# Remainder splits of the value and gate operands moved from GpSimd (POOL) to VectorE (DVE) in a two-layer decoder trunk

## The chip, the cores and the metric

The kernel runs on one core of one Trainium2 chip. The metric is the device time of one execution in microseconds (us). Engines are named as the profile names them: PE is TensorE (matmul), PEld its weight load, DVE is VectorE, ACT is ScalarE, POOL is GpSimd, SP is SyncE, which issues most DMAs. For a run of this kernel, about 0.3% (some 5.3 us) is what a measurement can tell from no change.

## The reference

The input x is 1024 tokens by 1024 features, float32. Layer 0 is an RWKV-7 time mixing, layer 1 a differential attention; each is followed by a gated per-layer embedding, and one RMSNorm ends the trunk. What matters here, cut down:

```
h = rms_norm(x);  dx = token_shift(h) - h
xm[g] = h + dx * mu[g]                      # g = r, k, v, gate
r, k, v, gate = xm[g] @ w_in[g]             # 1024x1024 each
...                                         # decay, per-head state update, group norm
x = x + (y * silu(gate)) @ w_out
x = x + sigmoid(rms_norm(x) @ pe_w_gate[0]) * (p[0] @ pe_w_proj[0])
...                                         # layer 1: differential attention
x = x + sigmoid(rms_norm(x) @ pe_w_gate[1]) * (p[1] @ pe_w_proj[1])
out = rms_norm(x)
```

## The kernel before

A matmul here is made of three in a shortened float type (float32r): an operand a is split into a main part (a rounded to float32r) and a remainder (a minus the main part), and a·b is taken as main·main + main·remainder + remainder·main (`mm3`, L90). `split` (L86) makes both: ACT writes the main part, and then POOL, or DVE where the caller says so, subtracts to get the remainder.

The work around the change, in order of time:

- **Mixed operands.** `make_xm` (L251) makes one 128x512 piece of xm[g]: ACT or DVE scales hT into a scratch tile `xmt` (a ring of 3), DVE adds the shifted part, `split` writes main part and remainder. There are 16 pieces for each g (8 feature blocks kt by 2 token halves). In the code g counts 1 for k, 0 for r, 2 for v, 3 for the gate. The remainder goes to DVE for kt 1, 4, 7 of v and kt 1 of the gate, and else to POOL.
- **Weights.** `wload` (L267) fetches a 128x1024 row of weights and splits it, always with POOL. The names are wv00 to wv31 for the 8 rows of v, and w0_, w1_, w3_ for the 8 rows each of r, k and the gate (w3_ is the gate; the profile prints these as w_0 to w_7).
- **Dense products.** `dense_T` (L274) makes k, then r; the loop at L681 makes v (4 column quarters by 8 token tiles, tiles `v`), and `dense_T` again makes the gate (tiles `d`). At the end of each dense product the operands of the next are made.
- **The inverse beside v and gate.** `inv_steps` (L646) runs in the background of v and gate. For four quarters q it makes products `pb` on PE, scales them on DVE (`nq`), transposes them on DVE (`nb`), and then does 31 steps of two DVE instructions each, one after the other (`tm`, then `tb`); two DVE transposes (`ea`, `ti`), copies on ACT (`prhs`, `pairs`) and small PE products (`pg`, `po`) end it.
- **The state update and layer 1** follow (from about 565 us); the order on the engines is pinned there by hand, and the edits do not touch it.
- **The last stage.** While layer 1's output projection runs (tiles `do`), `gate_pair` (L1551) fetches the 8 rows of the last gate's weights (pwg10 to pwg17) through `gate_row` (L761) and `wrow` (L743). Each row is scaled by a norm weight. With an engine given, `wrow` scales the raw row in place on ACT, then splits it: ACT main part, that engine the remainder. With none, ACT makes the main part with the scale in one instruction, and DVE makes the remainder with the scale in one instruction (SCALAR_TENSOR_TENSOR). The last token tile's chain (`os`, `ost`, `o`, `g`) runs beside it, and then the last gate's products (`fg`) begin.

Outside the pinned part the order of the instructions on each engine is set when the kernel is built, by a planner that simulates the program; each engine then runs its own list in order. Raw weight rows go through rings of two tiles, so the fetch of a row waits until the remainder two rows before it is made.

Of the kernel before, what the change touches and what calls it, by code (L numbers as in the profile page):

```python
# [37 lines left out]
def trunk(ctx: ExitStack, tc: tile.TileContext, A, out):  # L38
# [17 lines left out]
    V, S, G, T = engines = [Engine(e) for e in (nc.vector, nc.scalar, nc.gpsimd, nc.tensor)]  # L56
# [29 lines left out]
    def split(hi, lo, src, lo_eng=None):  # L86
        S.activation(hi, src, AF.Copy)
        (lo_eng or G).tensor_tensor(out=lo, in0=src, in1=hi.bitcast(F32), op=ALU.subtract)
# [132 lines left out]
    with NB("ab") as ab, NP("psab") as pp:  # L221
# [18 lines left out]
        def xslot(nm, n=512):  # L240
            return (ab.tile([P, 513], F32R, tag="xmh", name=nm + "h", bufs=XB)[:, 0:n],
                    ab.tile([P, 513], F32R, tag="xml", name=nm + "l", bufs=XB)[:, 0:n])

        def wraw(nm):
            return ab.tile([P, D], F32, tag="wr", name=nm, bufs=2)

        def wpair(nm):
            return (ab.tile([P, D], F32R, tag="wh", name=nm + "h", bufs=3),
                    ab.tile([P, D], F32R, tag="wl", name=nm + "l", bufs=3))

        def make_xm(g, kt, hf):  # L251
            h, lo = xslot(f"xm{g}_{kt}_{hf}")
            t = ab.tile([P, 512], F32, tag="xmt", name=f"xmt{g}_{kt}_{hf}", bufs=3)
            hc = hT[:, kt, hf * 512 + 1:hf * 512 + 513]
            if kt % 2 and g != 3:
                V.tensor_scalar(out=t, in0=hc, scalar1=cA[:, g, kt:kt + 1], scalar2=None, op0=ALU.mult)
            else:
                S.activation(t, hc, AF.Copy, scale=cA[:, g, kt:kt + 1])
            V.scalar_tensor_tensor(out=t, in0=hT[:, kt, half(hf)], scalar=cB[:, g, kt:kt + 1], in1=t,
                                   op0=ALU.mult, op1=ALU.add)  # L260
            split(h, lo, t, V if kt % (2 if g == 1 else 3 if g != 3 else 8) == 1 else G)
            return h, lo

        def make_half(g, hf):
            return [make_xm(g, kt, hf) for kt in range(KT)]

        def wload(nm, src):  # L267
            r = wraw(nm + "r")
            nc.sync.dma_start(out=r, in_=src)
            h, lo = wpair(nm)  # L270
            split(h, lo, r)
            return h, lo

        def dense_T(g, src, xm, ev, nxt, tick=lambda: None):  # L274
            new = [None, None]
            for jp in range(KT // 2):
                w = [wload(f"w{g}_{2 * jp + q}", src[2 * jp + q].rearrange("p k c -> p (k c)")) for q in range(2)]
                for hf in range(2):
                    for q in range(2):
                        ps = pp.tile([P, 512], F32, tag="mm", name=f"d{g}{2 * jp + q}{hf}", bufs=4)  # L280
                        for kt in range(KT):
                            cs = slice(kt * P, (kt + 1) * P)
                            mm3(ps, w[q][0][:, cs], w[q][1][:, cs], *xm[hf][kt], kt == 0, kt == KT - 1)
                            if kt % 2 and kt < KT - 1:
                                tick()
                        ev(2 * jp + q, hf, ps)
                        tick()
                    if nxt is not None and jp == KT // 2 - 1:
                        new[hf] = make_half(nxt, hf)
            return new  # L290
# [3 lines left out]
        with NB("pl") as pl:  # L294
# [56 lines left out]
            for nm, cf in (("c", cA), ("p", cB)):  # L351
                t = wraw("lw" + nm).rearrange("p (k c) -> p k c", c=P)
# [4 lines left out]
                h, lo = wpair("lws" + nm)  # L357
# [6 lines left out]
        with NB("cpool") as cpl:  # L364
# [8 lines left out]
            with NB("lo") as lw:  # L373
# [7 lines left out]
                def sgt(nm):  # L381
                    return lw.tile([P, D], F32, tag="sg", name=nm, bufs=2)

                r = sgt("w2r")
# [7 lines left out]
                def lora(hf):  # L392
                    ps = pp.tile([P, 512], F32, tag="mm", name=f"hid{hf}", bufs=4)
                    for kt in range(KT):
                        cs = slice(kt * P, (kt + 1) * P)
                        h, lo = hs[hf][kt]
                        for sh in range(2):
                            o = slice(1 - sh, 513 - sh)
                            mm3(ps, lws[sh][0][:, cs], lws[sh][1][:, cs], h[:, o], lo[:, o],
                                kt == 0 and sh == 0, kt == KT - 1 and sh == 1)  # L400
                    early_xm = [make_xm(1, kt, hf) for kt in range(NX)]
                    t = ab.tile([P, 512], F32, tag="xmt", name=f"hidt{hf}", bufs=3)
                    S.activation(t[0:L], ps[0:L], AF.Tanh)
                    hh = half(hf)
                    S.copy(hid1[0:L, hh], t[0:L])
                    S.copy(hidw[0:L, hh], t[0:L])
                    V.tensor_tensor(out=hidw[L:P, hh], in0=t[0:L], in1=hid1[0:L, hh].bitcast(F32), op=ALU.subtract)
                    S.copy(hida[L:P, hh], ps[L:P])
                    V.tensor_tensor(out=hida[0:L, hh], in0=ps[L:P], in1=hida[L:P, hh].bitcast(F32), op=ALU.subtract)
                    return early_xm  # L410
# [28 lines left out]
                for hf in range(2):  # L439
                    xm[hf] += [make_xm(1, kt, hf) for kt in range(NX, KT)]  # L440
                    for i in range(4):
                        decay(4 * hf + i)
                    if hf == 0:
                        a2_parts()
# [236 lines left out]
        for q in range(4):  # L681
            wv = [wload(f"wv{q}{k2}", A["wv"][q, k2].rearrange("p k c -> p (k c)")) for k2 in range(2)]
            for i in range(NT):
                x_ = xm[i // 4]
                ts_ = slice((i % 4) * P, (i % 4 + 1) * P)
                ps = pp.tile([P, 512], F32, tag="mm", name=f"v{q}{i}", bufs=4)[:, 0:256]
                for kt in range(KT):
                    if kt == 4 and (q or i > 3):
                        tick(TV)
                    cs = slice((kt % 4) * 256, (kt % 4) * 256 + 256)  # L690
                    mm3(ps, x_[kt][0][:, ts_], x_[kt][1][:, ts_], wv[kt // 4][0][:, cs], wv[kt // 4][1][:, cs],
                        kt == 0, kt == KT - 1)
                st = ab.tile([P, 512], F32, tag="xmt", name=f"vst{q}{i}", bufs=3)[:, 0:256]
                S.copy(st, ps)
                nc.sync.dma_start(out=v_d[i * P:(i + 1) * P, q * 256:(q + 1) * 256], in_=st)
                if q or i > 2:
                    tick(TV)
                if q == 3 and i % 4 == 3:
                    new[i // 4] = make_half(3, i // 4)
# [61 lines left out]
    def gate_row(ly, kt, own=None, eng=None, raw=None, load=True):  # L761
        return wrow(f"pwg{ly}{kt}", A["pwg"][ly, :, kt], own, vec[f"pe{ly}"][:, kt:kt + 1], eng, raw, load)
# [558 lines left out]
    with tc.tile_pool(name="at", bufs=1, reuse_waits="tile") as at, tc.tile_pool(name="psat", bufs=1, space=PSUM, reuse_waits="tile") as pp:  # L1321
# [226 lines left out]

        wg1 = []

        def gate_pair(kt, tags, eng=G):  # L1551

            own = None
            if tags == "k1":
                t = at.tile([P, 2, SEQ], F32R, tag="k1", name=f"wg1{kt}", bufs=2)
                own = (t[:, 0], t[:, 1])
            elif tags == "kv":
                own = (at.tile([P, SEQ], F32R, tag="k2", name=f"wg1{kt}h", bufs=2),
                       at.tile([P, SEQ], F32R, tag="vh", name=f"wg1{kt}l", bufs=2))
            elif tags == "q1":  # L1560
                own = (q1[:, 0], q1[:, 1])
            wg1.append(gate_row(1, kt, own, eng))
# [3 lines left out]
        def step(ph, ah, i):  # L1566
# [36 lines left out]
            else:  # L1603
# [7 lines left out]
                if i in (3, 5, 7):  # L1611
                    gate_pair(len(wg1), {3: "k1", 5: "kv", 7: "k1"}[i])
                if i == 7:
                    gate_pair(3, "q1")
# [15 lines left out]
            f()  # L1630
        emm(NT - 1, 1)
        for kt in range(4, KT):
            gate_pair(kt, None, G)
        fin = at.tile([P, D], F32, tag="e", name="fin", bufs=3)
        nc.sync.dma_start(out=fin, in_=A["fnorm"].to_broadcast([P, D]))
        nf = [0]
# [113 lines left out]
```

## Time and profile before

| | |
|---|---|
| median of 3 runs | 1774.21 us (1773.93 to 1779.56) |
| the profiled execution: its own time | 1772.86 us |
| its span, first to last instruction | 1770.7 us |
| PE busy | 1674.5 us (95%) |
| DVE busy | 1269.7 us (72%) |
| ACT busy | 797.5 us (45%) |
| POOL busy | 538.8 us (30%), 617 instructions |
| granted TensorE clock, mean | 0.964 |

Busy shares are means over the whole span. The stages differ, so the rows further down are cut by stretch: the operands of v are made at 291 to 325 us, v and gate run beside the inverse until about 565 us, and the last stage is at 1540 to 1680 us. A matmul's busy time is modelled, and a busy PE need not be a PE at its peak.

### The profile page before, as it was taken

To read this page: it belongs to the slowest core of one execution; us is meant where nothing else is said; L and a number is where in the kernel's file an instruction comes from. 1 tells how busy PE (TensorE), PEld (TensorE's weight loads), DVE (VectorE), ACT (ScalarE), POOL (GpSimd) and SP (SyncE) were. 2 spreads that over 40 slices of the span, in tenths; PEclk is the share of its full clock that TensorE was granted. 3 is DMA by queue.
4 is the path that set the end of the run, shared out by engine and by line. 5 is a ranking of instruction groups with operands and counts; after the bars stand their busy time and mean duration, and the time that the engine had idled before them with its cause. 6 is when DMAs were issued, how large, how long until landed. Compare 5 with 4: busy or idle time off the path is not lost.

```text
span 1770.7 us, 31132 instructions
## 1 busy us (share of the span) xinstructions
PE 1674.5 (95%) x11768; PEld 1393.3 (79%) x11768; DVE 1269.7 (72%) x2940; ACT 797.5 (45%) x1690; POOL 538.8 (30%) x617
## 2 busy tenths in 40 slices
PE   6899999898998999999899999999999999999998
PEld 5677778888677877888678788788888888787786
DVE  7875854697995367765856657887888888856665
ACT  6567843336445343334423433443444444543332
POOL 4533634214413555566400022222222222211200
PEclk9999999998899989998999999999999999999999
DMA  7115444433315654444523410110101101521122
GB/s 264 54 47 174 131 124 109 128 105 93 105 48 162 188 179 126 133 146 136 202 101 126 142 60 7 54 43 22 58 30 34 57 8 57 193 68 35 60 96 72
DMA packets 164404, 176.03 MB, mean 99 GB/s; under 512 B 74845, under 2 KB 127837, under 8 KB 164254
## 3 DMA queue, kind: packets, MB, share of 16 engines
q1 hardware_dynamic: 161950, 169.84, 30.8%
q10 hardware_dynamic: 2304, 4.20, 0.6%
q8 instruction: 93, 1.52, 0.4%
q14 instruction: 57, 0.47, 0.1%
HBM read 124.19 MB, written 49.81 MB: 98 GB/s over the span
## 4 chain that ended last, share of the span: by engine, by line
PE 58%; DVE 26%; issue 5%; ACT 5%; POOL 3%; DMA 3%; SPq 0%; ACTq 0%; DVEq 0%; POOLq 0%
PE qkv L50 15%; PE d L50 6%; PE fg L50 5%; PE do L50 5%; PE pg L50 5%; DVE xmt L50 3%; PE xy L50 3%; DVE tm L50 3%; PE op L50 3%; DVE tb L50 3%; PE sc L50 3%; PE av L50 3%; DVE nb L50 2%; PE pm L50 1%; POOL m L50 1%
## 5 line engine op out<-in xcount | busy, mean ns | idle before, releaser
L50 ACT ACTIVATE e<-sc,mx 128x256 f32<-128x256 f32 (+7 forms) x128 | 94.1, 738 | 106.7 <-DVE mx L50 70.9
L50 POOL TENSOR_TENSOR rp<-rp,rq 128x128 f32<-128x128 f32 x128 | 61.5, 501 | 203.8 <-DVE rq L50 79.0
L50 PE MATMUL sc<-k,q 128*128 128x512 f32 (+2 forms) x384 | 88.8, 362 | 3.3 <-ACT e L50 3.3
L50 PEld LDWEIGHTS av<-vh,aT 128*128 128x128 f32 x576 | 74.7, 191 | 13.1 <-DVE aT L50 4.2
L50 PE MATMUL av<-vh,aT 128*128 128x128 f32 x576 | 78.6, 277 | 5.4 <-ACT o L50 2.9
L50 DVE TENSOR_REDUCE mxs<-sc 128x1 f32<-128x128 f32 (+6 forms) x112 | 73.8, 680 | 0.9
L50 PE MATMUL do<-dwo,oh 128*128 128x512 f32 x224 | 72.3, 404 | 2.2 <-ACT oh L50 1.7
L50 PE MATMUL pg<-pwg,ph 128*128 128x512 f32 x224 | 73.7, 408 | 0.0
L50 POOL CAST q<-q 64x128 fp32r<-64x128 f32 x128 | 38.6, 302 | 113.4 <-PE sc L50 110.1
L50 POOL TENSOR_TENSOR m<-m,mmask 128x512 f32<-128x512 f32 x32 | 47.8, 1494 | 82.1 <-ACT m L50 82.1
L50 PEld LDWEIGHTS sc<-k,q 128*128 128x128 f32 x384 | 63.2, 189 | 12.0 <-ACT e L50 4.4
L50 POOL CAST k<-k 64x256 fp32r<-64x256 f32 x64 | 29.6, 462 | 130.3 <-ACT k L50 99.6
L50 DVE SCALAR_TENSOR_TENSOR xmt<-hT,cB,xmt 128x512 f32<-128x512 f32 x64 | 63.6, 1010 | 6.1 <-ACT xmt L50 5.8
L50 ACT ACTIVATE o<-av,r 128x128 f32<-128x128 f32 x64 | 23.4, 366 | 97.9 <-PE av L50 97.8
L50 DVE TENSOR_TENSOR tm<-tb,nb 128x31 f32<-128x31 f32 (+15 forms) x124 | 56.1, 452 | 3.6
L50 DVE TENSOR_TENSOR rp<-qkv,rc 128x256 f32<-128x256 f32 x64 | 27.0, 421 | 41.9 <-PE qkv L50 36.7
L50 DVE TENSOR_TENSOR tb<-tb,tm 128x31 f32<-128x31 f32 (+15 forms) x124 | 52.8, 426 | 3.6
L50 DVE SCALAR_TENSOR_TENSOR e<-e,r,e 128x128 f32<-128x128 f32 (+3 forms) x64 | 53.8, 841 | 1.2
L50 DVE COPY aT<-at 128x512 f32<-128x512 f32 (+2 forms) x96 | 51.9, 549 | 1.9 <-PE at L50 1.5
L50 DVE TENSOR_TENSOR m<-pm,mmask 128x512 f32<-128x512 f32 x32 | 22.1, 692 | 41.3 <-PE pm L50 41.2
L50 PEld LDWEIGHTS do<-dwo,oh 128*128 128x128 f32 x224 | 41.6, 191 | 11.7 <-ACT oh L50 2.0
L50 PEld LDWEIGHTS pg<-pwg,ph 128*128 128x128 f32 x224 | 42.3, 193 | 9.3 <-ACT ph L50 0.2
(1136 smaller groups left out, 5546.5 us busy)
## 6 DMA issues: line engine op xcount, KB each, us to landing
pp_d<-ppo SPq DMA_DIRECT2D x32, 256.0 KB, 2.3
kb_d<-kb SPq DMA_DIRECT2D x16, 512.0 KB, 3.3
kkr<-kkr_d SPq DMA_DIRECT2D x32, 256.0 KB, 3.5
kb<-kb_d SPq DMA_DIRECT2D x32, 256.0 KB, 3.4
x<-in_x SPq DMA_DIRECT2D x8, 512.0 KB, 4.9
kkr_d<-ep SPq DMA_DIRECT2D x16, 256.0 KB, 2.6
kkr_d<-rt SPq DMA_DIRECT2D x16, 256.0 KB, 2.6
bb<-kb_d SPq DMA_DIRECT2D x32, 128.0 KB, 3.2
```

The lines of the kernel that those rows point to most:

```text
L50: r = f(*a, **k)
```

## The change

Three edits, each of which takes subtractions from POOL. In `make_xm` every remainder of v's and the gate's mixed operands is made on DVE (10 pieces of v and 14 of the gate change engine; those of k and r stay as they were). In `wload` the remainders of v's 8 weight rows and of the gate's 8 rows are made on DVE. In `gate_pair` no engine is given, so that the 8 rows of the last gate take `wrow`'s last branch.

```diff
-            split(h, lo, t, V if kt % (2 if g == 1 else 3 if g != 3 else 8) == 1 else G)
+            split(h, lo, t, V if g > 1 or kt % (2 if g == 1 else 3) == 1 else G)
...
-            split(h, lo, r)
+            split(h, lo, r, V if nm[:2] in ("wv", "w3") else G)
...
-        def gate_pair(kt, tags, eng=G):
+        def gate_pair(kt, tags, eng=None):
...
-            gate_pair(kt, None, G)
+            gate_pair(kt, None)
```

## Rows read from the trace of the kernel before

**Rows 1.** Windows: length; busy us of PE, PEld, DVE, ACT, POOL; granted clock; DMA.

```profile
291.00:325.00 34.00, 29.10 (x202) 25.67 (x201) 31.46 (x31) 16.20 (x26) 20.31 (x12) 0.99 0.28 68
...
340.00:420.00 80.00, 76.60 (x858) 74.55 (x857) 75.66 (x146) 29.79 (x54) 18.10 (x10) 0.96 0.43 118
420.00:440.00 20.00, 14.01 (x252) 13.06 (x254) 12.16 (x17) 18.09 (x28) 10.50 (x10) 0.85 0.30 68
...
455.00:543.00 88.00, 81.78 (x489) 62.37 (x489) 85.24 (x152) 34.32 (x54) 24.75 (x16) 0.88 0.22 71
```

**Rows 2.** Chain of waits, 340 to 543 us: shares by engine and tile.

```profile
by line: DVE tm L50 26.8%; DVE tb L50 25.1%; DVE nb L50 14.8%; issue 6.4%; DVE ge L50 5.1%; DVE ea L50 4.4%; DVE xmt L50 3.9%; DVE nq L50 3.4%; ACT prhs L50 3.0%; DVE ti L50 1.8%; ACT xmt L50 1.4%; ACT xm_0h L50 1.2%; ACT ti L50 1.0%; ACT p
```

**Rows 3.** PE's waits, 285 to 575 us: total us, times, longest.

```profile
PE pb L50 <- DVE nq L50: 5.6, 3, 3.1
PE pg L50 <- ACT prhs L50: 5.1, 3, 3.2
PE v L50 <- ACT vst L50: 4.9, 1, 4.9
PE po L50 <- ACT prhs L50: 4.2, 2, 2.6
```

**Rows 4.** DVE's groups by shape, 291 to 325 us: busy us, mean ns | idle before.

```profile
L50 DVE SCALAR_TENSOR_TENSOR xmt<-hT,cB,xmt 128x512 f32<-128x512 f32 x13 | 14.1, 1111 | 0.2
L50 DVE TENSOR_SCALAR xmt<-hT,cA 128x512 f32<-128x512 f32 x7 | 10.0, 1431 | 0.1
L50 DVE TENSOR_TENSOR xm_0l<-xmt,xm_0h 128x512 fp32r<-128x512 f32 x3 | 3.5, 1163 | 1.4 <-ACT xm_0h L50 1.3
...
L50 DVE TENSOR_TENSOR xm_1l<-xmt,xm_1h 128x512 fp32r<-128x512 f32 x3 | 2.1, 688 | 0.8 <-ACT xm_1h L50 0.8
```

**Rows 5.** DVE's timeline, 291 to 455 us: start, us, instruction.

```profile
294.09 1.53 DVE L50 TENSOR_SCALAR xmt<-hT,cA 128x512 f32<-128x512 f32 x1
...
296.98 0.48 DVE L50 TENSOR_SCALAR xmt<-hT,cA 128x512 f32<-128x512 f32 x1
...
437.24 0.75 DVE L50 SCALAR_TENSOR_TENSOR xmt<-hT,cB,xmt 128x512 f32<-128x512 f32 x1 [4.16 <-ACT xmt L50]
...
439.59 8.10 DVE L50 STREAM_TRANSPOSE nb<-nq 32x1024 f32<-32x1024 f32 x4
```

**Rows 6.** POOL's timeline, 435 to 455 us.

```profile
439.36 2.53 POOL L50 TENSOR_TENSOR w_1l<-w_1r,w_1h 128x1024 fp32r<-128x1024 f32 x1 [0.24 <-ACT w_1h L50]
```

**Rows 7.** DVE's groups by shape, whole span: three of the inverse's 62 steps.

```profile
L50 DVE TENSOR_TENSOR tb<-tb,tm 128x252 f32<-128x252 f32 x8 | 8.6, 1078 | 0.2
...
L50 DVE TENSOR_TENSOR tm<-tb,nb 128x252 f32<-128x252 f32 x8 | 7.5, 943 | 0.2
...
L50 DVE TENSOR_TENSOR tm<-tb,nb 128x255 f32<-128x255 f32 x8 | 3.4, 422 | 0.2
```

**Rows 8.** DVE's groups by shape: row remainders where POOL is quiet (1450 to 1545, 860 to 910).

```profile
L50 DVE TENSOR_TENSOR dwo<-dwo0r,dwo 128x1024 fp32r<-128x1024 f32 x1 | 1.2, 1217 | 0.0
...
L50 DVE SCALAR_TENSOR_TENSOR pwg<-pwg06r,vecs,pwg 128x1024 fp32r<-128x1024 f32 x1 | 1.3, 1284 | 0.0
```

**Rows 9.** Last stage, 1645 to 1670 us: timeline of DVE and POOL, then PE's wait.

```profile
1654.60 0.16 DVE L50 TENSOR_TENSOR ost<-ost 128x2 f32<-128x2 f32 x1
...
1655.19 2.26 DVE L50 TENSOR_TENSOR ost<-ost 128x2 f32<-128x2 f32 x1
1657.49 2.47 DVE L50 SCALAR_TENSOR_TENSOR ost<-ost 128x2 f32<-128x2 f32 x2
...
1655.00 2.43 POOL L50 TENSOR_TENSOR pwg<-pwg14r,pwg 128x1024 fp32r<-128x1024 f32 x1 [41.55 <-ACT pwg L50]
...
PE o L50 <- DVE o L50: 3.3, 1, 3.3
```

**Rows 10.** ACT's groups by shape, 1540 to 1680 us: one of eight scalings in place.

```profile
L50 ACT ACTIVATE pwg14r<-pwg14r,vecs 128x1024 f32<-128x1024 f32 x1 | 1.1, 1149 | 5.4 <-DMA pwg14r<-in_pwg 5.4
```

**Rows 11.** DVE's groups by shape, 420 to 475 us: wait of its one remainder there.

```profile
L50 DVE TENSOR_TENSOR xm_0l<-xmt,xm_0h 128x512 fp32r<-128x512 f32 x1 | 1.7, 1716 | 2.2 <-ACT xm_0h L50 2.2
```

## The prediction, made before the changed kernel was run

> **What bounds the kernel now.** PE is busy 95% of the span, but the edits lie where it is short of work, so I read by stretch: first the windows, then the chain of waits, then PE's waits, and last the groups of DVE by shape, where the price of the edits stands.
>
> The windows [rows 1] show DVE as the fullest engine in both stretches of the first part: 31.46 of 34 us while v's operands are made, 75.66 of 80 and 85.24 of 88 beside the inverse; only from 420 to 440 is it idle for 7.8 us, and there ACT is full (18.09 of 20). The chain from 340 to 543 says the same: over half is the inverse's two alternating instructions tm and tb, and most of the rest is DVE too [rows 2]. PE pays with waits of 4.9 us (for v's second half of operands; the last to end before it is a copy of v, but that copy was queued behind the operands on ACT) and 5.6 + 5.1 + 4.2 = 14.9 us for products of the inverse [rows 3]. So DVE, not PE, sets the pace until 543 us.
>
> The reader should then see that DVE's work there is stretched. The same instruction, TENSOR_SCALAR on 128x512, takes 1.53 us at 294.09 and 0.48 us at 296.98 [rows 5]; tm and tb on 252 columns take 943 and 1078 ns on average, on 255 columns 422 [rows 7]. What differs is a POOL subtraction running at the same time. Not every DVE instruction suffers: the four transposes at 439.59 take 8.10 us together [rows 5], 2.03 us each, although POOL's 2.53 us weight row covers the first of them [rows 6]; a wait until that row ended would have made the first alone over 4 us. So a POOL subtraction is paid for on DVE when it meets an elementwise instruction on two SBUF operands or a scaling, and free beside a transpose.
>
> **The change, part by part.** On a quiet DVE a remainder of 128x512 costs 0.69 us (that of the second token half [rows 4]), of 128x1024 1.22 us, with the scale in it 1.28 us [rows 8].
>
> *Operands of v, 291 to 325 us.* Removed from POOL: 10 remainders of operands and 2 weight rows (wv01, wv10), all its 20.31 us there [rows 1]. Added to DVE: 10 x 0.69 + 2 x 1.22 = 9.3 us. Taken off DVE: the stretching, 13 x (1.111 - 0.75) = 4.7 us on the additions, 7 x (1.431 - 0.48) = 6.7 us on the scalings, 3 x (1.163 - 0.69) = 1.4 us on its own remainders [rows 4, 5], 12.8 us in all. Net -3.5 us on the chain that PE waits 4.9 us for, so PE can take all of it. Bounds: -4.9 (wait gone) and +1 (only half the stretching goes, 6.4 against 9.3, less 2 of DVE's idle time). I take -3.5, the middle of the rows. wv00, earlier, lies in DVE's idle time.
>
> *Beside the inverse, 340 to 543 us.* Added to DVE: 14 x 0.69 = 9.7 us for the gate's operands, and 13 weight rows (five of v, eight of the gate) x 1.22 = 15.9 us, together 25.6. Taken off: the two rows of 252 columns give 8 x (1.078 - 0.42) + 8 x (0.943 - 0.42) = 9.4 us [rows 7]; eight further groups of the same view (60 to 247 columns), raised in the same way against a twin of their size, give about 14.8 by the same working, and 16 additions and one remainder about 3: 27 us. Net -1.6. Of what is added, five remainders (3.5 us) fall between 420 and 440, where DVE idles 7.8 us, so the chain gets up to 5 us shorter. PE is about 93% busy and more beside most of it [rows 1] and can win only part of its 14.9 us of waits; I take -2.5. Bounds: -6 and +4 (the POOL work beside the transposes, four weight rows and two remainders, was free: 4 x 1.22 + 2 x 0.69 = 6.3 us that buy nothing, against 2.5).
>
> *Where the order matters.* DVE runs its list in order. A remainder that waits for ACT's main part holds up everything behind it, the inverse's next step above all. And raw weight rows pass through rings of two, so a later remainder makes SP fetch the next row later; a POOL row took 2.53 us and a DVE row takes 1.22, so that queue gains unless the remainder stands behind a long transpose.
>
> *Last gate's rows, 1540 to 1680 us.* ACT loses eight in-place scalings of 1.15 us [rows 10], off the path. POOL loses eight subtractions, DVE gains 8 x 1.28 us. Six of them lie beside PE-bound matmuls and cost nothing: DVE has room, and PE waits for no such row. Two, rows 14 and 15, lie in the last token tile's chain: there two tiny DVE instructions (128x2) take about 2.3 us each beside POOL's 2.43 [rows 9], where a neighbour of theirs takes 0.16; some 4.2 us of stretching, and PE waits 3.3 us for that chain [rows 9]. Afterwards the two remainders cost 2.6 us if they stand inside the chain (net -1.6) and nothing if they stand before or behind it (-3.3). I take -2.5. Cover for the last two rows are the first `fg` products, which use them late; if that fails, up to 1.3 us each.
>
> **The sum:** -3.5 - 2.5 - 2.5 = -8.5 us. The profiled execution took 1772.86 us (span 1770.7 and 2.2 around it), 1.35 under the median of the runs; so 1764.4 on its own scale and about **1765.5 us** beside the median of 1774.21.
>
> **A rule against it.** DVE is 97% busy from 455 to 543 us [rows 1], and the change gives it 25.6 us more beside the inverse. The Trainium skill, "Perfetto Trace Analysis", section "Optimizing Scalar/DVE Operations", advises offloading some work to ScalarE or even GpSimd when DVE is saturated, the reverse of this change; it adds that the two share a read port, so that it might not help. By its first half alone the sum would be the full price, the rival "full DVE" below; by the rows above most of the price is already being paid.
>
> **The rivals.**
> 1. *Waits at the head of DVE's list (slower).* Place: 420 to 475 us, where the gate's operands are made and ACT is full. DVE's one remainder of the first half there waited 2.2 us for its main part [rows 11]. If seven do, that is 15.4 us, 7.8 of them idle before: +7.6; if all fourteen do, 30.8 - 7.8 = +23. With the gains of the other two parts kept (1768.0) that gives 1775.6 to 1791, say 1783. It turns slower by over 0.3% once the mean wait passes about 1.4 us (14 x 1.4 - 7.8 = 11.8). For it: PE's first gate products depend on these pieces, and the planner must place twice as many DVE instructions. Against: two or three pieces are in work at once, and the planner sees ACT's times. Chance 0.17.
> 2. *Hidden (no change).* What DVE saves beside the inverse is lost in the next wait for ACT or in PE's own full stretches, and v's operands gain only half: -1.7 - 0 - 2.0, so 1770.5 us. For it: PE is 93% busy from 455 to 543 [rows 1]. Chance 0.23.
> 3. *The clock comes back too (faster still).* The granted clock is 0.85 from 420 to 440 and 0.88 from 455 to 543 [rows 1], that is 30% and 24% of the time at the lower level (1.2 of 2.4 GHz), in stretches in which PE waited before. That is up to 0.15 x 20 + 0.12 x 88 = 13.6 us of work at full rate. If half returns with the waits: 1758.5. Chance 0.17.
> 4. *Full DVE.* The stretching stays and the work is added: +9.3 and 25.6 - 3.5 = 22.1 us, about 1805. It would need the stretching to have another cause than POOL. Chance 0.03.
> 5. *It does not do what it says.* The order that the planner finds was the limit, and POOL's share was not: 1774. The operands of k and r, and their 16 weight rows, stay on POOL anyway. Chance 0.02.
>
> **How the numbers follow.** The forecast has 0.38, its own range is 1760 to 1768.5. Faster by over 0.3% (5.3 us, below 1768.9): the forecast and rival 3, 0.55. Within 0.3%, about what a measurement of this kernel can tell from no change: rivals 2 and 5, 0.25. Slower: rivals 1 and 4, 0.20. The range goes from 1757, rival 3 with its bound, to 1779, the lower part of rival 1.
>
> **What would show it.** Right: POOL has no instruction from 291 to 325 us, and DVE's scalings there take 0.48 us and its additions 0.75 throughout; PE's wait of 4.9 us shrinks to 1 or 2; tm and tb of 252 columns fall to about 0.42 us; DVE's busy time from 340 to 543 stays within 3 us; the 128x2 instructions at the end take 0.16 to 0.18 us, and PE's wait for `o` is under 1.7 us. Wrong: waits of DVE for main parts that sum to over 12 us around the gate's operands; a clock that falls further; new waits of PE for remainders of weight rows; or an unchanged chain through tm and tb although each is shorter, which would mean that another engine had set the pace.

## The result, and the profile after

The changed kernel takes **1760.18 us** (median of 5 runs, 1757.21 to 1764.48), against 1774.21 for five runs of the kernel before taken beside it: a ratio of 0.9913, 95% interval [0.9893, 0.9933]. It is faster, by 14.0 us where 8.7 were forecast: inside the range, and at the lower edge of the forecast's own (1760 to 1768.5). The profiled execution has a span of 1758.4 us (before: 1770.7). The sum was too small: it had left out what the clock gives back, and it did not have what is lost again behind the edits.

The windows of the kernel after, for the stretches of [rows 1]:

```profile
291.00:325.00 34.00, 34.00 (x266) 30.12 (x265) 27.62 (x46) 18.17 (x29) 0.00 (x0) 1.00 0.39 99
340.00:420.00 80.00, 76.40 (x896) 73.15 (x895) 76.09 (x167) 37.52 (x65) 3.00 (x4) 1.00 0.45 121
420.00:440.00 20.00, 15.29 (x163) 11.25 (x161) 19.62 (x25) 12.74 (x22) 3.02 (x4) 0.94 0.38 101
455.00:543.00 88.00, 83.99 (x626) 67.74 (x624) 72.55 (x150) 37.39 (x58) 10.15 (x15) 0.96 0.30 98
```

While v's operands are made POOL has nothing left, DVE does 46 instructions in 27.62 us instead of 31 in 31.46, and PE goes from 29.10 busy us of 34 to all 34 with 64 matmuls more. From 340 to 440 us DVE does 192 instructions where it did 163; from 455 to 543 us it does about as many as before (150 and 152) in 12.7 us less.

Fixed windows hold different work in the two kernels. From 285 us to the first matmul of the state update (`xy`) they hold the same, but for a few matmuls; the kernel before, then the kernel after:

```profile
285.00:574.70 289.70, 263.87 (x2330) 227.54 (x2328) 233.74 (x389) 131.59 (x214) 93.91 (x65) 0.92 0.38 106
...
285.00:554.50 269.50, 252.35 (x2332) 218.82 (x2331) 224.00 (x429) 132.92 (x214) 23.53 (x27) 0.95 0.41 114
```

The stretch is 20.2 us shorter. PE's idle time in it falls by 8.7 us (25.8 to 17.2), and its busy time by 11.5 for about the same matmuls. That is the clock: by the trace's clock records 44.8 us of the busy time lay at the lower level (1.2 GHz) before and 23.2 after (26.4 in a second execution of the kernel after, `after_again` below). The gate's matmuls follow one another every 0.43 us at the lower level and every 0.23 us at the higher, so this is worth about 10 us of the 11.5 (8 in the second execution).

DVE's groups by shape, 291 to 325 us, against [rows 4]:

```profile
L50 DVE SCALAR_TENSOR_TENSOR xmt<-hT,cB,xmt 128x512 f32<-128x512 f32 x13 | 9.6, 746 | 0.0
L50 DVE TENSOR_TENSOR xm_0l<-xmt,xm_0h 128x512 fp32r<-128x512 f32 x8 | 5.5, 688 | 0.7 <-ACT xm_0h L50 0.7
L50 DVE TENSOR_SCALAR xmt<-hT,cA 128x512 f32<-128x512 f32 x7 | 3.4, 482 | 0.0
```

and over the whole span the two groups of the inverse, against [rows 7]:

```profile
L50 DVE TENSOR_TENSOR tb<-tb,tm 128x252 f32<-128x252 f32 x8 | 3.4, 421 | 0.2
L50 DVE TENSOR_TENSOR tm<-tb,nb 128x252 f32<-128x252 f32 x8 | 3.3, 418 | 0.1
```

Additions 746 ns (1111 before), scalings 482 (1431), steps of the inverse 421 and 418 (1078 and 943): the stretching is gone, to the nanoseconds forecast. The instructions are the same; what ran beside them changed, and their order with it.

PE's waits, 285 to 575 us, against [rows 3]:

```profile
PE po L50 <- ACT prhs L50: 4.5, 4, 2.2
PE d L50 <- ACT xm_1h L50: 3.3, 1, 3.3
...
PE v L50 <- DVE wv31l L50: 1.2, 1, 1.2
PE v L50 <- DVE wv11l L50: 1.1, 1, 1.1
...
PE pg L50 <- ACT prhs L50: 0.8, 1, 0.8
```

The wait of 4.9 us in v is gone, as are those for `nq`; two small ones for weight remainders, now queued in DVE's list, have come, and one of 3.3 us for a main part of the gate's operands (0.3 before). The chain from 340 to 543 us, against [rows 2], has changed hands: DVE's tm and tb were 52% of it, and PE's own products (`d`, `v`) now lead it.

```profile
by line: PE d L50 26.4%; PE v L50 17.1%; DVE nb L50 10.4%; issue 6.0%; DVE tb L50 3.7%; PE po L50 3.4%; DVE tm L50 3.3%; DVE ea L50 3.2%; ACT pairs L50 2.9%; DVE ge L50 2.8%; ACT prhs L50 2.8%; DVE ti L50 2.8%; PE pb L50 2.8%; DVE xmt L50 2
```

**Where the time came from and where it went** is best seen by landmarks: the start or end of the same instruction in each profiled execution (us from the span's start).

| landmark | before | after | difference |
|---|---|---|---|
| v's 97th matmul | 324.5 | 319.9 | -4.6 |
| last matmul of v | 429.7 | 417.8 | -12.0 |
| first matmul of the gate | 441.2 | 417.7 | -23.5 |
| last matmul of the gate | 564.8 | 538.6 | -26.2 |
| last product of the inverse (`po`) | 558.5 | 541.5 | -17.0 |
| first matmul of the state update (`xy`) | 574.7 | 554.5 | -20.2 |
| first matmul of layer 1 (`qkv`) | 1002.8 | 982.9 | -19.9 |
| ninth `rq`, after layer 1's first head | 1059.8 | 1044.6 | -15.2 |
| last `qkv` | 1528.9 | 1514.9 | -14.0 |
| first product of the last gate (`fg`) | 1667.3 | 1654.8 | -12.5 |
| end | 1770.7 | 1758.4 | -12.3 |

The gain is made between 291 us and the gate's last matmul, and about half of it is given back: about 6 us by 575 (the gate is 26 us early, the inverse only 17, and the state update needs both), about 5 us in the first head of layer 1, which no edit touches, and some 3 us spread behind that.

The loss in layer 1's first head has a row of its own. DVE's waits, 1000 to 1062 us, of the kernel after:

```profile
DVE rp L50 <- PE qkv L50: 13.9, 4, 6.0
DVE hT4l L50 <- ACT hT4h L50: 5.2, 1, 5.2
```

and the two rows that stand for it before:

```profile
DVE rp L50 <- PE qkv L50: 8.5, 4, 3.9
DVE rp L50 <- PE qkt L50: 4.7, 1, 4.7
```

In the kernel after a remainder `hT4l` stands in DVE's list ahead of work that was ready, and waits 5.2 us for ACT. The planner's lists differ there from before's in 13 or 14 places each on PE, DVE and ACT, though the program text of that part is the same.

The last stage, against [rows 9]: DVE's timeline from 1642 us, then PE's wait.

```profile
1642.69 0.16 DVE L50 SCALAR_TENSOR_TENSOR ost<-ost 128x2 f32<-128x2 f32 x1
1642.93 1.28 DVE L50 SCALAR_TENSOR_TENSOR pwg<-pwg14r,vecs,pwg 128x1024 fp32r<-128x1024 f32 x1
1644.14 0.15 DVE L50 SCALAR_TENSOR_TENSOR ost<-ost 128x2 f32<-128x2 f32 x1
1644.21 1.28 DVE L50 SCALAR_TENSOR_TENSOR pwg<-pwg15r,vecs,pwg 128x1024 fp32r<-128x1024 f32 x1
1645.40 0.15 DVE L50 TENSOR_TENSOR ost<-ost 128x2 f32<-128x2 f32 x1
1645.94 0.69 DVE L50 TENSOR_TENSOR h<-do,h 128x512 f32<-128x512 f32 x1 [0.38 <-PE do L50]
...
PE o L50 <- DVE o L50: 2.3, 1, 2.3
```

The tiny instructions are back to 0.15 us, but both row remainders, and an `h` addition with its wait, now stand inside their chain. PE's wait fell by 1.0 us only.

### The profile page after: what moved, and what is told of

Its sections match the earlier page's. It is cut to its first block, busy times and chain, and to the rows that moved or that the text cites. A ratio compares the mean times of both kernels' runs of the same rounds, so it can differ in the third digit from the quotient of the medians.

```text
span 1758.4 us, 31106 instructions
## 1 busy us (share of the span) xinstructions
PE 1665.9 (95%) x11768; PEld 1384.6 (79%) x11768; DVE 1261.6 (72%) x2988; ACT 791.3 (45%) x1682; POOL 444.3 (25%) x569
## 4 chain that ended last, share of the span: by engine, by line
PE 68%; DVE 16%; issue 4%; ACT 4%; DMA 4%; POOL 3%; SPq 0%; DVEq 0%; ACTq 0%; POOLq 0%
PE qkv L50 17%; PE d L50 10%; PE fg L50 5%; PE do L50 5%; PE pg L50 5%; PE xy L50 3%; PE sc L50 3%; PE v L50 3%; PE op L50 3%; PE av L50 3%; DVE xmt L50 2%; PE pm L50 2%; DVE nb L50 1%; POOL m L50 1%; PE pps L50 1%
## 5 line engine op out<-in xcount | busy, mean ns | idle before, releaser
L50 PEld LDWEIGHTS sc<-k,q 128*128 128x128 f32 x384 | 63.0, 189 | 15.6 <-ACT e L50 6.1
L50 ACT ACTIVATE o<-av,r 128x128 f32<-128x128 f32 x64 | 23.5, 366 | 96.7 <-PE av L50 96.5
L50 POOL MEMSET tb<- 128x1024 f32 (+1 forms) x8 | 4.5, 559 | 212.7 <-DVE ti L50 200.7
L50 DVE SCALAR_TENSOR_TENSOR xmt<-hT,cB,xmt 128x512 f32<-128x512 f32 x64 | 57.1, 907 | 0.4 <-ACT xmt L50 0.2
L50 PEld LDWEIGHTS do<-dwo,oh 128*128 128x128 f32 x224 | 41.4, 191 | 12.5 <-ACT oh L50 3.0
```

The costliest lines, as they stand in the source:

```text
L50: r = f(*a, **k)
```

## The experiments

The theory after the result: (a) POOL's subtractions stretch DVE's work, and the gain comes from their removal; (b) what is given back is not a price of DVE's added work but of lists that the planner wrote anew. The main rival to (a): the edits act through the order of the lists alone. In each batch the kernel before ran on the same chip; ratios are to it.

### The edits one at a time

Edits 1 (mixed operands), 2 (weight rows) and 3 (last gate's rows) alone, each the hunks of the diff that stand ahead; edit 3 is the hunks of `gate_pair`:

```diff
 xm_only
+            split(h, lo, t, V if g > 1 or kt % (2 if g == 1 else 3) == 1 else G)
 w_only
+            split(h, lo, r, V if nm[:2] in ("wv", "w3") else G)
 gate_only
+        def gate_pair(kt, tags, eng=None):
+            gate_pair(kt, None)
```

> Only the mixed operands' remainders go to DVE (10 of v, 14 of the gate); weight rows and the last gate stay on POOL. Port theory (a POOL subtraction blocks DVE's two-operand and scaling instructions while it runs): POOL keeps some 38 us of weight rows, so DVE's scalings at 291 to 325 us are clean except beside wv01 and wv10, PE's wait for v's second half falls from 4.9 to under 2.5 us, and the inverse's tm and tb are still stretched beside the weight rows; 1763 to 1768 us, about half of the whole change's 14. Latency theory (what counts is that a remainder is ready in 0.7 instead of 1.5 us, and PE waits for operands): nearly all of the gain, 1759 to 1762, since only these pieces are waited for by PE.

> Only the 16 weight rows of v and the gate go to DVE. Port theory: the inverse's steps beside wv21 to w_7 lose their stretching (about 17 us) and DVE gets 16 x 1.22 = 19.5 us, of which some 4 lie in idle time: 1767 to 1773 us. Latency theory: weight rows are fetched early and nobody waits for them, so nothing is gained and the work lengthens DVE: 1774 to 1780 us.

> Only the last gate's rows change. Port theory as predicted: PE's wait for the last token tile's o falls from 3.3 to about 1 us, -2.5 us: 1771 to 1773 us. Rival (the two remainders stand inside the chain on DVE and take what the stretching took): within 1 us of the kernel before, 1773 to 1775 us, and the wait stays over 2 us.

| kernel | median (range) | before | ratio [95%] | first gate matmul | first `xy` | first `qkv` | first head |
|---|---|---|---|---|---|---|---|
| before | | 1772.65 | | 441.2 | 574.7 | 1002.8 | 57.0 |
| edit 1 | 1769.63 (1762.09 to 1773.45) | 1772.65 | 0.9975 [0.9956, 0.9995] | 433.7 | 566.3 | 994.6 | 59.0 |
| edit 2 | 1769.28 (1765.42 to 1777.76) | 1772.65 | 0.9993 [0.9976, 1.0009] | 433.2 | 567.1 | 994.2 | 60.5 |
| edit 3 | 1771.66 (1768.59 to 1778.04) | 1772.65 | 0.9999 [0.9985, 1.0013] | 441.5 | 577.1 | 998.3 | 57.7 |

("First head" is the ninth `rq` less the first `qkv`.) Edits 1 and 2 alone each bring the gate's first matmul forward by 8 us and each give most of it back behind 995 us; in the end edit 1 is worth 0.25%, less than the 0.3% that a measurement can tell, and edit 2 nothing that can be told. (The landmarks are of single executions; that of edit 1, with 1772.43 us, is one of the slowest of its twelve.) Edit 1's median lies outside both of its expected ranges, edit 2's in that of the port theory. POOL is still busy for 48 us (edit 1) and 44 us (edit 2) between 285 us and 10 us before the gate's end, against 89 before and 9 after. Edit 3 is worth nothing; PE's wait for `o` is 2.3 us with it, as its rival had it.

### Edits 1 and 2 together

> Both edits of the v and gate part, without that of the last gate's rows. Alone the first was worth about 3 us, the second about 1, all three together 14. If the two need each other (one POOL subtraction left in the stretch is enough to hold the inverse's chain, and each edit alone only moves the wait), 1759 to 1763 us. If each is worth what it was worth alone and the missing rest came from the last gate's rows, 1767 to 1771.

1759.97 us (1757.09 to 1762.88) against 1774.19, 0.9915 [0.9895, 0.9935]: the full result without edit 3. The first gate matmul comes at 419.9, that is 21.3 us early where the two alone make 7.5 and 8.0. From the first `do` to the first `fg` the last stage takes 129.6 us before, 130.2 after, 129.9 here, and 128.8 with edit 3 alone. So edit 3 adds nothing here and at most 0.9 us alone, and 1 and 2 are worth more together than apart.

### Unused work on POOL, and the same on DVE

The kernel after with 32 subtractions that nobody reads, 16 while v's operands are made and 16 while the gate's are, each on POOL (`pool_extra`) or each on DVE (`dve_extra`):

```diff
             split(h, lo, t, V if g > 1 or kt % (2 if g == 1 else 3) == 1 else G)
+            if dum:
+                G.tensor_tensor(out=dum[0], in0=hT[:, kt, hf * 512:hf * 512 + 384], in1=h.bitcast(F32)[:, 0:384], op=ALU.subtract)
```

> The changed kernel, and for each piece of v's and the gate's mixed operands one more POOL subtraction of 128x384 (32 in all, about 1.1 us each) from two SBUF operands into a tile that nobody reads; no instruction of another engine waits for it. Port theory: DVE's scalings and two-operand instructions beside them are stretched again, by 0.5 to 1 us each: 8 to 20 us back, 1768 to 1780 us. Latency or order theory: POOL's work is off every path, so no change, 1758 to 1763 us.

> The changed kernel with the same 32 unused subtractions of 128x384 as in the run with more POOL work, but on DVE (about 0.5 us each, 17 us in all, half of them beside the inverse). Port theory: DVE pays their own time and no more, and part lies in its idle time: 1763 to 1769 us, clearly less than the 12 us that the same work cost on POOL. If DVE's load as such sets the time, all of it shows: 1774 to 1778. If PE has become the bound, nothing: 1758 to 1762.

On POOL: 1772.5 us (1768.98 to 1776.96), 0.9996 [0.9982, 1.0011] to a before of 1772.65: the gain is gone, 12.3 us more than the kernel after, though the lists of PE, DVE and ACT are instruction for instruction those of the kernel after, and POOL's too but for the 32. On DVE: 1766.55 us (1762.79 to 1771.23), 0.9957 [0.9943, 0.9972] to 1774.19: 6.4 us more. POOL's groups by shape in `pool_extra`, 285 to 545 us:

```profile
L50 POOL TENSOR_TENSOR dum<-hT,xm_0h 128x384 f32<-128x384 f32 x16 | 21.4, 1336 | 43.1 <-ACT xm_0h L50 42.5
L50 POOL TENSOR_TENSOR dum<-hT,xm_1h 128x384 f32<-128x384 f32 x16 | 21.2, 1324 | 29.7 <-ACT xm_1h L50 29.3
```

DVE's groups in `pool_extra`, 291 to 325 us:

```profile
L50 DVE SCALAR_TENSOR_TENSOR xmt<-hT,cB,xmt 128x512 f32<-128x512 f32 x12 | 10.8, 909 | 0.0
L50 DVE TENSOR_TENSOR xm_0l<-xmt,xm_0h 128x512 fp32r<-128x512 f32 x8 | 8.5, 1060 | 0.7 <-ACT xm_0h L50 0.7
L50 DVE TENSOR_SCALAR xmt<-hT,cA 128x512 f32<-128x512 f32 x7 | 6.2, 884 | 0.0
```

and in `dve_extra`, the same stretch:

```profile
L50 DVE SCALAR_TENSOR_TENSOR xmt<-hT,cB,xmt 128x512 f32<-128x512 f32 x12 | 8.8, 746 | 0.0
...
L50 DVE TENSOR_TENSOR dum<-hT,xm_0h 128x384 f32<-128x384 f32 x8 | 4.4, 551 | 0.0
...
L50 DVE TENSOR_SCALAR xmt<-hT,cA 128x512 f32<-128x512 f32 x7 | 3.4, 480 | 0.0
```

Nothing waits for `dum`, nor does DVE wait for anything of POOL's between 285 and 555 us, yet DVE's neighbours rise to 909, 1060 and 884 ns beside it on POOL, and stay at 746 and 480 with 0.55 us more each on DVE. PE's waits in `pool_extra`, 285 to 545 us, show what that does:

```profile
PE v L50 <- ACT vst L50: 5.2, 1, 5.2
PE d L50 <- ACT vst L50: 4.3, 1, 4.3
```

The wait of 4.9 us [rows 3] is back at 5.2, and the gate begins with a new one. Its first matmul comes 13.0 us later than in the kernel after (430.8 against 417.7), the first `xy` 15.1 us; up to that `xy` PE's idle time is back at 26.2 us, where before had 25.8 and after 17.2. This settles (a) against its rival: with no list changed, **work on POOL that nobody needs costs the kernel 12 us**. How much of DVE's time it takes is read by comparing every DVE instruction with the same one in the kernel after: 9.3 us from 285 to 325 us and 8.4 from there to 540 us, 17.7 in all or 0.55 for each subtraction, and the same on DVE takes 0.55. So a subtraction on POOL beside DVE is not free at all; here it took as much of DVE's time as making it there.

That the medians differ (12.3 against 6.4) is not settled by this. `dve_extra` has other lists: its first head is in before's order and takes 56.6 us, not 61.7, and its entry to the state update (from the last `po` to the first `xy`) takes 17.1 us, not 13.0, with POOL's list there in the order that `order_back` shows below. To its first gate matmul it is 6.2 us later than the kernel after, to its first `xy` 15.2.

The Trainium skill, "SBUF — State Buffer", section "SBUF: two separate sides", gives in its account of the shared port pair a cause: DVE and GpSimd (POOL) take it as an exclusive lock for a whole instruction, also where DVE reads two SBUF operands while GpSimd reads SBUF, and the later one blocks. The 2.26 us of a 128x2 instruction beside POOL's 2.43 [rows 9] agree with blocking, and so do the ends of the stretched instructions (last section); that it is this lock no run here can show.

### The order of layer 1's first head

One change to the kernel after: the gate's block kt 0 (two pieces) stays on POOL, after which the planner writes before's order again for the first head, on PE, DVE and ACT alike. `r_too` also takes r's operands and rows to DVE, so that beside that block only k's stay on POOL (of them the even kt; k's odd kt and r's kt 1, 4 and 7 were on DVE from the start).

```diff
 order_back
-            split(h, lo, t, V if g > 1 or kt % (2 if g == 1 else 3) == 1 else G)
+            split(h, lo, t, V if g > 1 and (g, kt) != (3, 0) or g < 2 and kt % (2 if g == 1 else 3) == 1 else G)
 r_too
-            split(h, lo, t, V if g > 1 or kt % (2 if g == 1 else 3) == 1 else G)
+            split(h, lo, t, V if g != 1 and (g, kt) != (3, 0) or g == 1 and kt % 2 == 1 else G)
-            split(h, lo, r, V if nm[:2] in ("wv", "w3") else G)
+            split(h, lo, r, V if nm[:2] != "w1" else G)
```

> The changed kernel, but two of the gate's 14 pieces (kt 0) keep their remainder on POOL. By the planner's list of instructions this brings back the order that the kernel before has in the first head of layer 1, while v and gate keep theirs of the changed kernel but for some places. If that order costs what the traces show between the first head's start and the second's (2.6 to 5 us): 1755 to 1759 us. If the loss there comes from arriving earlier (transfers that are late), the order is no matter: 1760 to 1764.

> As the run before, and r's mixed operands and weight rows are made on DVE as well (only k's stay on POOL). Port theory: DVE is stretched by some 17 us between 180 and 240 us in the kernel before, but PE waits only 3.1 us there: 1 to 4 us better than the run before, 1752 to 1757 us. Rival (DVE, fuller by 20 us, makes r's products late): 1757 to 1765.

`order_back`: 1761.59 us (1758.9 to 1763.15), 0.9923 [0.9904, 0.9943]; no faster than the kernel after. The first head did come back: 56.8 us, before's 57.0, where the kernel after takes 61.7. But the time from the last `po` to the first `xy` became 21.6 us (before 16.2, after 13.0), and took it all: the order does cost what its expectation said, and another order ate the gain. `r_too`: 1756.54 us (1751.39 to 1764.24), 0.9899 [0.9872, 0.9927]: v begins 4.9 us earlier than in `order_back` (302.6 against 307.5), as in v's own case: DVE's additions (`xmt`) from 180 to 240 us take 798 ns on average, not 1245, and PE's waits of 3.0 us between 180 us and v's start are gone. The entry is again 21.6 us. POOL's timeline of `order_back` at that entry, and PE's:

```profile
541.39 1.06 POOL L50 TENSOR_TENSOR spl<-state,plast 128x512 f32<-128x512 f32 x1 [8.15 <-DMA sg_d<-ge]
545.41 5.72 POOL L50 TENSOR_TENSOR wpl<-wp,wph 128x1024 fp32r<-128x1024 f32 x2 [2.96 <-ACT wph L50]
551.10 1.04 POOL L50 TENSOR_TENSOR kbp<-kb,plast 128x512 f32<-128x512 f32 x1
...
552.20 1.12 PE L50 MATMUL kbt<-ident,kbp 128*128 128x128 f32 x4 [11.25 <-POOL kbp L50]
```

The planner has put two weight remainders (`wpl`, of the second embedding projection) ahead of `kbp` in POOL's list, and PE waits 11.25 us for `kbp`. In the kernel after they stand behind it. That is read from one row, and the next runs tried it.

### The two remainders at the entry taken off POOL

In `ple_load`, for layer 1's embedding, the remainder of `wp` goes to DVE, which is idle at the entry; on top of `order_back` (`ob_ple`) and of `r_too` (`r_ple`). The kernel after ran once more beside them (`after_again`).

```diff
-                split(h, lo, r, V if nm == "p" else G)
+                split(h, lo, r, V if nm == "p" or ly == 1 else G)
```

> The kernel order_back with the two remainders of the second embedding weight (wpl, 128x1024) at the entry to the state update made on DVE, which is idle there, in place of POOL. In order_back POOL's list has these two (5.72 us, with 2.96 us of waiting for ACT's main parts) ahead of kbp, which PE's kbt products wait for; kbp starts at 551.10. Theory 1 (POOL's list order sets the entry): kbp starts at about 542.5, the time from the last po to the first xy falls from 21.6 us to about 13, and the median by 6 to 8 us, to about 1754. Theory 2 (the loads set it: SP's queue fetches kb and kkr behind sg_d, and POOL's place is covered by them): kbp or kbt wait for a DMA in POOL's place, the entry stays at 19 to 22 us, median 1760 to 1763.

> The kernel r_too with the same two remainders on DVE. r_too gained 5 us at v's start over order_back and had the same entry (21.6 us). Theory 1: 6 to 8 us less than r_too, median about 1749, the fastest of all. Theory 2: no change, 1756 to 1757.

> The changed kernel itself once more, on the same chip as the two above, for comparison. Both theories: 1760, ratio 0.991 to before; entry to the state update 13.0 us, and 5 us lost in layer 1's first head.

| kernel | median (range) | ratio to before (1772.8) [95%] | last `po` to first `xy` | first head | end of span |
|---|---|---|---|---|---|
| ob_ple | 1753.62 (1751.06 to 1757.62) | 0.9892 [0.9875, 0.9910] | 15.3 | 57.1 | 1749.3 |
| r_ple | 1748.56 (1741.79 to 1751.54) | 0.9856 [0.9833, 0.9880] | 15.3 | 56.9 | 1744.4 |
| after_again | 1761.77 (1759.32 to 1762.35) | 0.9930 [0.9915, 0.9945] | 13.0 | 62.7 | 1760.5 |

Both medians are 8.0 us below those without the edit, which ran in the batch before on another chip; by the ratios it is 5.5 and 7.6 us. The kernel after repeats its result and its long first head, and **r_ple is the fastest of all, 13.2 us below the kernel after on the same chip**; part of that may be the clock, with a mean of 0.971 granted in its runs against 0.968. POOL's timeline at the entry in `ob_ple`, then PE's:

```profile
542.59 1.06 POOL L50 TENSOR_TENSOR spl<-state,plast 128x512 f32<-128x512 f32 x1 [8.16 <-DMA sg_d<-ge]
543.60 1.05 POOL L50 TENSOR_TENSOR kbp<-kb,plast 128x512 f32<-128x512 f32 x1
547.39 2.02 POOL L50 TENSOR_TENSOR kbp<-kb,plast 128x512 f32<-128x512 f32 x1
...
544.71 1.11 PE L50 MATMUL kbt<-ident,kbp 128*128 128x128 f32 x4 [2.58 <-POOL kbp L50]
```

PE's 11.25 us are 2.58. The second `kbp` comes 3.8 us after the first (two `pr`, a wait of 1.06 us for a load of `kb`) and takes 2.02 us, not 1.05, beside DVE's new remainder (546.76 to 548.51): in this row the stretching works in the other direction too. So the entry stays 2 us above the kernel after's. In the profiled executions, which stand 11.4 us apart, the entry gives 6.3 of it and the state update itself 5.0. The latter goes with the clock rather than with the edit: PE's, DVE's and ACT's lists there are those of `order_back`, PE is busy for 399.8 us instead of 406.8 with about the same matmuls at a granted clock of 0.95 instead of 0.94, and `gate_only`, whose lists there are before's, differs from before in the same way (421.2 us instead of 428.1, at 0.96 instead of 0.93). So the two remainders are worth about 6 us by the traces.

## Why the prediction was right, and where it was not

- **The mechanism (POOL's subtractions stretch DVE's work): shown.** The durations fell to the forecast values; `pool_extra` gave POOL other subtractions to do with the lists unchanged, and longer durations, waits and the old time came back with them. Rival 4 (full DVE) falls: with 27 subtractions more beside the inverse, DVE's busy time from 340 to 543 us went from 187.6 to 181.8 us, 5.8 down where 1.6 was the sum, though not with the same work in the window. On the same work (operands of v and gate, their weight rows, the inverse) it went from 240.7 to 236.1, 4.6 down where the two parts of the sum had 3.5 + 1.6; the steps tm and tb alone lost 24.1 us, where 9.4 + 14.8 were put. Rivals 2 and 5 fall with the gain and with `pool_extra`. The Trainium skill, "Perfetto Trace Analysis", section "Optimizing Scalar/DVE Operations", advises offloading a full DVE; its own reservation about the shared port was what counted.
- **Operands of v, -3.5 us: right.** v's 97th matmul comes 4.6 us earlier, inside the bounds of -4.9 and +1; PE's idle time from 285 us up to it went from 4.9 us to nothing.
- **Beside the inverse, -2.5 us: right for the waits; the failed step is the clock, put at nothing.** Between v's 97th matmul and the first `xy` the kernel after gains 15.6 us (-20.2 less -4.6), far outside the bounds of -6 and +4. The step read "PE is about 93% busy and more beside most of it and can win only part of its 14.9 us of waits", and this came: PE's idle time there fell by 3.8 us (20.9 to 17.2), inside the bounds. The other 11.8 us are busy time, 229.3 against 217.5 us for 2104 and 2112 matmuls, at a granted clock of 0.90 and 0.94. The sum had no term for that; it stood apart, as rival 3.
- **Where the order shows.** Between the last matmul of v (429.7) and the first of the gate (441.2) lie 11.5 us. PE did products of the inverse for 5.7 of them, which it has to do somewhere, and was idle for 5.8 (two of the waits in [rows 3]), at a granted clock of 0.68. DVE came to the gate's operands only at 421.55 us, behind the second quarter's transposes, and ACT then made their main parts in between the inverse's copies, busy for 11.1 of the 11.5 us. After, DVE makes the first at 407.07 us, in among the quarter's last steps, and the gap is zero (417.8 and 417.7). The first of these operands in DVE's timeline of the kernel before:

```profile
421.55 1.31 DVE L50 SCALAR_TENSOR_TENSOR xmt<-hT,cB,xmt 128x512 f32<-128x512 f32 x2
```

  and after, between two of the inverse's steps:

```profile
406.85 0.30 DVE L50 TENSOR_TENSOR tm<-tb,nb 128x135 f32<-128x135 f32 x1
407.07 0.75 DVE L50 SCALAR_TENSOR_TENSOR xmt<-hT,cB,xmt 128x512 f32<-128x512 f32 x1
407.73 0.29 DVE L50 TENSOR_TENSOR tb<-tb,tm 128x135 f32<-128x135 f32 x1
```

  So part of the gain is a new order too: in `pool_extra`, with these lists and POOL at work again, the gap is 4.3 us, between 11.5 and 0. How much of the 20.2 us is order and how much stretching is not separated by that.
- **Rival 1 (waits at the head of DVE's list at the gate's operands): fell where it was put.** DVE's group there, 400 to 440 us, against [rows 11]:

```profile
L50 DVE TENSOR_TENSOR xm_0l<-xmt,xm_0h 128x512 fp32r<-128x512 f32 x8 | 5.5, 693 | 0.0
```

  Eight remainders, no wait for ACT's main parts; all of DVE's waits for main parts of v's and the gate's operands and weight rows sum to 3.3 us, where over 12 was the sign of being wrong. But the same mechanism struck where I had not looked, at `hT4l` in layer 1's first head (5.2 us), for the list there was written anew. `order_back` shows it: before's order gives 4.9 us back.
- **Rival 3 (the clock comes back too): came, beside the forecast.** The granted clock rose from 0.85 to 0.94 and from 0.88 to 0.96. Up to the first `xy` it gave about 10 us (8 in `after_again`) of the 13.6 that could have come. Over the whole execution PE's busy time is 8.6 us shorter (1674.5 and 1665.9), so of the 12.3 us that remain at the end 3.7 are idle time. Some of this is the luck of the profiled executions: the mean granted clock of all runs is 0.966 before (61 runs) and 0.968 after (10 runs), about 3 us of work. Nor is it shown that the clock follows PE's idle time: in `dve_extra` PE is idle longest up to the first `xy` (30.6 us), and as little of its busy time (21.1 us) lies at the lower level as in the kernel after.
- **Last gate's rows, -2.5 us: wrong, nothing measurable.** The two remainders stand inside the chain, the case put at "(net -1.6)", with an `h` addition beside them; PE's wait went from 3.3 to 2.3, and the stage as a whole is no shorter (130.2 us against 129.6). I had taken a value between the two cases; `xm_w` loses nothing without the edit.
- **Not foreseen:** what is given back. The gate's last matmul is 26.2 us early, but the inverse's last `po` only 17.0, and the state update starts behind the later of the two; and the planner's new list costs 5 us at 1000 to 1060 us. So the sum -8.5 came near the -12.3 of the profiled execution by two errors against one another: 20.2 us gained up to the state update, where 6.0 were summed, and some 8 us of it lost behind, where 2.5 more were to be gained. That the time fell inside the range is luck in this respect.
- **Why edits 1 and 2 are worth more together:** the gate's first matmul comes 8 us earlier with each and 21.3 with both; alone each leaves half of POOL's work beside DVE's. What each alone loses behind 995 us was read from the landmarks and not tried.

## What to carry to other kernels

Before taking work off a full engine, look at the same instruction's duration with and without its neighbour: where a POOL subtraction stretches the DVE instructions beside it, moving it onto DVE can lower DVE's own busy time. When a gain is read, split it over the same work into idle time and busy time of the engine that sets the pace: here 8.7 of 20.2 us were waits, and 11.5 the same matmuls at a higher granted clock, a term that the sum had left out. And where a planner writes the lists, compare every engine's list over the whole program after an edit: here reordering in two places that no edit touched was worth 5 and about 6 us, and undoing both, with r's work moved as well, beat the change by 13 us.

## What the runs showed of the hardware that was not expected

- A POOL subtraction that nobody waits for is as dear for DVE as its own: 0.55 us of DVE's time for each 128x384 on POOL, 0.55 for one made on DVE; 32 of them on POOL cost the kernel 12.3 us.
- For those DVE instructions that suffer, the price goes by the POOL instruction and not by their own size: a 128x2 instruction of 0.16 us took 2.26 beside POOL's 2.43 [rows 9]. One of the inverse's steps in the kernel before, with POOL's row ahead of it:

```profile
402.14 2.68 POOL L50 TENSOR_TENSOR wv31l<-wv31r,wv31h 128x1024 fp32r<-128x1024 f32 x1 [17.35 <-PE v L50]
...
402.59 2.51 DVE L50 TENSOR_TENSOR tm<-tb,nb 128x252 f32<-128x252 f32 x1
407.65 0.42 DVE L50 TENSOR_TENSOR tm<-tb,nb 128x247 f32<-128x247 f32 x1
```

  The step ends 0.28 us after POOL's row (405.10 and 404.82). From 285 to 545 us of that trace 33 scalings and instructions on two SBUF operands of DVE start while a POOL subtraction runs, and 32 of them end 0.15 to 0.56 us after it.
- Which kind suffers: six transposes that start beside a POOL subtraction in the same stretch kept their 2.0 us, and so did, at 0.41 and 0.68 us, six instructions with a matmul's result as one operand (`nq<-pb,rn` and `rt<-d,rt`).
